# Experts of a mixture-of-experts layer: four with 32 slots share the tensor engine's array

## The chip, the cores and the metric

The kernel runs on one core of one Trainium2 chip. The metric is the device time of one execution in microseconds (us). In the text PE is the tensor engine (PEld its loading of weights), DVE the vector engine, ACT the scalar engine, POOL GpSimd and SP the sync engine, whose queue issues nearly all loads here.

## The reference

The reference is one decoder layer for 512 tokens of 1024 features: token mixing (HGRN2 and NSA attention, merged and projected), then a layer norm, then a hierarchical mixture of experts, then a layer norm. The change lies in the mixture of experts. Each token picks one of 4 groups and two of the 8 experts in it, and each of the 32 experts is a SwiGLU network from 1024 features to 512 and back:

```
(jax.nn.silu(xb @ w1[e]) * (xb @ w3[e])) @ w2[e]
```

There are 512 x 2 = 1024 choices. Routing the reference's inputs by its own rule gives experts 0 to 3 38, 37, 51 and 29 tokens; the other 28, sorted, have 81, 57, 49, 46, 41, 40, 37, 37, 35, 33, 33, 32, then 30, 30, 29, 29, 29, 27, 25, 24, 20, 19, 18, 16, 16, 14, 12, 10. An expert's three matrices are 2 MB each in float32, so that all 32 experts are 201 MB, read once.

## The kernel before

The first 760 us compute token mixing, the first norm and the router. The rest goes through the experts in **units** of 128 slots. A slot holds one token of one expert. Units -2 and -1 are experts 0, 1 and 2, 3 with 64 slots each. The other experts are sorted by their count of tokens on the chip (`sort_experts`, lines 1371 to 1431): ranks 0 and 1 have 128 slots each and are units 0 and 1 alone; ranks 2 to 27 have 64 slots each and run two to a unit, units 2 to 14. In all there are 17 units: 15 of two experts ("pairs" below) and 2 of one ("singles"). Their order is the list `ORDER` (line 75).

For each unit the loop in lines 1549 to 1578 writes out, in this order on PE: `up` (the products with w1 and w3, tile `p`); `combine` of the unit before (16 products `pcb`, which carry its rows back to the tokens); after each second unit `gather` for the next two units (64 products `pgx`, which pick the tokens' rows); transposes `pat` and `ptw`; and `down` (products with w2, tile `py`). In a pair the two experts' products stand in the two halves of the array, columns 0 to 63 and 64 to 127, by `tile_position` (line 1449). All unit products are float32; the program's one product is two matmul instructions in the trace.

SP loads each expert's weights as 12 tiles `ew` of 512 KB, four for each matrix, in the order in which PE uses them: within a unit, tile by tile and for each tile expert by expert (`load_unit`, lines 1250 to 1272). The tiles come from a pool of 36 buffers (line 158), of which 12 hold the tokens' rows and sums for the rest of the program. So 24 buffers go round: from the second unit on, each load takes the buffer of the 24th load before it, and waits until PE has made the last product with that tile. The loads also wait in turn for the one eight places before. For a unit of sorted experts SP reads each expert's number from the sorted list `ovi` (function `ev`, line 1513).

Tokens past an expert's slots go through `overflow` (line 1516), a loop over blocks of 128 slots, whose count is known only on the chip; the trace of before has no instruction of its body. The last unit's w2 comes in quarters of columns (line 1267), and its `down` and `combine` are interleaved by quarters with the sums for the last norm (lines 1637 to 1657). After that come the norm and the stores.

Of the kernel before, what the change touches and what calls it, by code (L numbers as in the profile page):

```python
# [27 lines left out]
OP = mybir.AluOpType  # L28
# [11 lines left out]
CAP = 64  # L40
SCALE = 128 ** -0.5

# columns of the constant array
# [3 lines left out]
def const_arrays():  # L47
    c = np.zeros((128, C_N), np.float32)
    p = np.arange(128)
    c[:, C_ID:C_ID + 128] = np.eye(128)  # L50
    c[:, C_TRI:C_TRI + 128] = p[:, None] <= p[None, :]
    c[:, C_IOTA:C_IOTA + 256] = np.arange(256)[None, :]
    c[:, C_VAL] = p >= 31
    # bias by distance: dist = 511 - m; bucket one-hot, then the mask row
    m = np.arange(640)
    dist = 511 - m
    n = np.maximum(dist, 1).astype(np.float64)
    large = np.minimum(16 + (np.log(n / 16) / math.log(8) * 16 + 1e-9).astype(np.int64), 31)
    bucket = np.where(np.maximum(dist, 0) < 16, np.maximum(dist, 0), large)
    oh = np.zeros((32, 1280), np.float32)  # L60
    ok = dist >= 0
    oh[bucket[ok], m[ok]] = 1.0
    oh[:, 640:] = np.where(ok, 0.0, NEG)[None, :]
    return {"cst": c, "buck": oh}
# [10 lines left out]
ORDER = [2, 3, 4, 0, 5, 6, 7, 1, 8, 9, 10, 11, 12, 13, 14]  # L75
# [4 lines left out]
class Weave:  # L80
    """Emission order: a main stream of products, with side streams put in between when what they
    wait for should be there by the tensor engine's clock."""
# [59 lines left out]
def hybrid_kernel(ctx, tc, a, out, dbg=None, stop=None):  # L142
# [52 lines left out]
    # rows 0..15 ada sh1, sc1; 16..23 c  # L195
# [6 lines left out]
    # rows 0..51 b_in[:6656]; 52..67 gates' biases; 68..83 lb logits; 84..91 norm_w; 92, 93 cmp_b1  # L202
# [7 lines left out]
    # second weights and positions of the two compressions  # L210
# [29 lines left out]
    def sigmoid(dst, src, nbias):  # L240
        # 1 / (1 + exp(-x)) as exp(-ln(1 + exp(-x)))
# [10 lines left out]
    class Block:  # L252
# [16 lines left out]
        def split1(self, sub=None):  # L269
# [3 lines left out]
            if self.early:  # L273
                # the branch's factor of each column
# [20 lines left out]
    def proj_T(b, c, ps, sh=None, sl=None, ks=range(KT)):  # L295
        # features on partitions, tokens along the free axis
# [19 lines left out]
    def run_jobs(jobs):  # L316
        """jobs: (block or None, body(block) -> generator, names of side streams to end before)"""
        blocks = [j[0] for j in jobs]

        def ahead(i):  # L320
            # what the next blocks still need, one piece at a time
# [70 lines left out]
    # layer norm of x, transposed  # L392
# [48 lines left out]
    # the first of each 32 rows: two of shift, two of scale  # L441
# [3 lines left out]
    def modulation(c):  # L445
        # 256 features of shift and scale, as rows: each over two halves of the products
# [8 lines left out]
    def modulate(c):  # L455
        # the same as columns, and their rows of h^T
# [33 lines left out]
    # lower bound: softmax over the two depth rows, row 0  # L490
# [16 lines left out]
    mod_d = dr.tile([1, 4096], F32, name="mod_d")  # L507

    def late_mod():
        accs = []  # L510
        for j in range(8):
# [13 lines left out]
            # rows side by side in the array  # L525
# [11 lines left out]
    # bias by distance, masked, as one row a head; its Toeplitz views are read back from DRAM  # L537
# [3 lines left out]
    def bias_rows():  # L541
# [23 lines left out]
        # row p of a head is read from 127 - p on: a step of 639 over 128 copies of the row  # L565
# [4 lines left out]
    # compressed values in two exact halves, stacked: high, low, high  # L570
    vcmp = cp.tile([96, 2, 128], F32R, name="vcmp")

    def compress(src, wname, b1, is_k):
# [20 lines left out]
        # windows on partitions, even and odd positions side by side  # L594
# [34 lines left out]
    # keys: per group [selected 512 | window 512], and the first blocks of both side by side  # L629
# [80 lines left out]
    def attention(hp, i):  # L710
# [55 lines left out]
        # probabilities with the keys on partitions: two blocks of keys, two heads a bank  # L766
# [18 lines left out]
        # of the compressed keys: high, high, low  # L785
# [58 lines left out]
    def c4(t):  # [128,512] as [p, tile, chunk, 32]  # L844
        return t.rearrange("p (i c j) -> p i c j", i=NT, c=4)

    def bc32(f):  # factor [128,16] over 32 tokens
# [7 lines left out]
    def hgrn_gates(h):  # L855
# [11 lines left out]
        # chunk decays and their products inside a tile of four chunks  # L867
# [3 lines left out]
        pr2 = fac[:, 5]  # [.., 0] d0 d1, [.., 1] d2 d3, [.., 2] all four  # L871
# [13 lines left out]
    def hgrn(h):  # L885
# [12 lines left out]
        # state updates  # L898
# [5 lines left out]
        # attention inside a tile, keys on partitions  # L904
# [55 lines left out]
    def on_split(hp):  # L960
        # after a pair's last tile
# [21 lines left out]
    def prep():  # L983
# [5 lines left out]
        # sh2, 1 + sc2: feature p * 8 + k on partition p  # L989
# [13 lines left out]
        # router weights with the modulation folded in  # L1003
# [91 lines left out]
    def out_piece(b, i, q, width):  # L1095
        # 256 of a tile's columns; added to x in pieces of width
# [23 lines left out]
    pk1, pk2 = S("pk1"), S("pk2")  # L1120
    onesb, strict = bfs[:, 0:128], bfs[:, 128:256]
    # scratch of [128, 4, 8] pieces
# [19 lines left out]
    def gather_first(tiles, ks=range(8)):  # L1142
        # the rows of experts 0..3: the first three tiles of tokens ahead of the last one's ranks;
        # one accumulation a bank: its second half starts where the first one's start has cleared
# [8 lines left out]
    def ln(i, z, st):  # L1153
# [32 lines left out]
        # what the experts need of the rows  # L1186
# [11 lines left out]
        # logits on partitions, even and odd features side by side  # L1198
# [9 lines left out]
        # group, two experts in it  # L1208
# [18 lines left out]
        # rank among the tokens of an expert  # L1227
# [7 lines left out]
        # slots of experts 0..3, 64 each  # L1235
# [14 lines left out]
    def load_unit(es, lo=0, hi=12, res=None, quarters=False):  # L1250
        res = res or {n: [[] for _ in es] for n in ("exp_w1", "exp_w3", "exp_w2")}
        for t in range(lo, hi):
            name = ("exp_w1", "exp_w3", "exp_w2")[t // 4]
            for x, e in enumerate(es):
                j = t % 4
                src = expert_rows(name, e)
                if t in SMALL and isinstance(e, int) and e < 2:
                    # two tiles of half the size: of those there are more than the start of the experts needs
# [6 lines left out]
                if quarters and t >= 8:  # L1265
                    # 256 columns of all rows
# [26 lines left out]
    # the routing of the last tile of tokens, the other tiles' rows in its waits  # L1293
# [25 lines left out]
    # combine weights: p(group) * softmax of the two  # L1319
# [12 lines left out]
    def one_hots(rels):  # L1332
        # rows of tokens, columns of two units' slots
# [9 lines left out]
    def gather(ph_):  # L1343
        # the rows of the slots, features on partitions, modulated
# [26 lines left out]
    def sort_experts():  # L1371
        # experts 0..3 have 64 each; of the others the two fullest have 128 and the rest 64
# [4 lines left out]
        key, rk, base, cap_, two, cnt = (srt[:, 32 * j:32 * j + 32] for j in range(6))  # L1377
# [7 lines left out]
        # the experts in the order of their units  # L1385
# [7 lines left out]
        def look(dst, table):  # L1393
            # by the expert of each choice
# [3 lines left out]
        # slots of the sorted experts  # L1398
        V.tensor_scalar(two, rk, 2.0, None, op0=OP.is_lt)
        V.tensor_scalar(cap_, two, 64.0, 64.0, op0=OP.mult, op1=OP.add)  # L1400
        V.tensor_scalar(base, rk, 64.0, -128.0, op0=OP.mult, op1=OP.add)
        V.tensor_mul(base, base, two)
        V.scalar_tensor_tensor(base, rk, 64.0, base, op0=OP.mult, op1=OP.add)
        V.tensor_scalar(base, base, 128.0, None, op0=OP.add)
# [7 lines left out]
        # tokens past an expert's slots: blocks of 128, one expert each  # L1412
# [4 lines left out]
        for j in range(1, 4):  # L1417
# [8 lines left out]
        le = S("le").rearrange("p (j e) -> p j e", j=16)  # L1426
        V.tensor_tensor(le, incl[:, None, :].to_broadcast([128, 16, 32]),
                        iota[:, 0:16].rearrange("p (j o) -> p j o", o=1).to_broadcast([128, 16, 32]), op=OP.is_le)
        V.tensor_copy(ovf[:, 32:33], incl[:, 31:32])
        V.tensor_reduce(ovf[:, 33:49].rearrange("p (j o) -> p j o", o=1), le, axis=AX.X, op=OP.add)  # L1430
        V.tensor_copy(ovi[:, 32:49], ovf[:, 32:49])

# [1 line left out]
    def weighted(rel):  # L1434
        # token rows, slot columns, weights of the choices
# [8 lines left out]
    def unit_mm(ps, lhs, n0, ws, rhs, nk):  # L1444
        # one expert, or two side by side in the array
# [36 lines left out]
    def weighted_halves(py, cs_, c0, n):  # L1482
        # columns from c0 on, weighted, in two exact halves
# [32 lines left out]
    def overflow():  # L1516
# [4 lines left out]
        with tc.For_i(0, nblk, 1) as jb:  # L1521
# [8 lines left out]
            def stream(name):  # L1530
                # a product's weights, used in the order of their loads
# [7 lines left out]
            # the last norm's sums so far  # L1539
# [5 lines left out]
    # units -2, -1: experts 0..3; 0, 1: one expert; 2..14: two  # L1545
# [3 lines left out]
    for n, u in enumerate(units):  # L1549
# [6 lines left out]
        if n == 4:  # L1556
            # of the tokens past an expert's slots
            nblk = nc.values_load_multi_w_load_instructions(
                ovi[0:1, 32:33], min_val=0, max_val=15, skip_runtime_bounds_check_because="a sum of at most 15 blocks")[1][0]
# [4 lines left out]
        if n + 1 < len(units):  # L1564
# [3 lines left out]
            elif v_ < 2:  # L1568
                es = (ev(v_),)
            else:  # L1570
                es = (ev(2 * v_ - 2), ev(2 * v_ - 1))
# [11 lines left out]
    aT, pT, cs_ = down_lhs(act, pw)  # L1583
    l3 = cp.tile([128, NT, 6], F32, name="l3")
    # sums of a tile's quarters; its halves' sums of squares, off by a shift (the first quarter's mean)
# [9 lines left out]
    def quarter_up(q):  # L1595
        # 256 columns of the last unit
# [8 lines left out]
    def quarter_add(q, y, i):  # L1605
        # the last two units' rows of a tile
# [15 lines left out]
    def close(i, half, how):  # L1622
        # norm, gain and offset of half a tile, by the engines of the three steps (two where fused)
# [34 lines left out]
    # mean; variance from the shift, less the square of what the shift missed  # L1658
# [40 lines left out]
```

## Time and profile before

| | |
|---|---|
| median of three timed runs | 1299.36 us (1298.15 to 1299.7) |
| span of the profiled execution, first to last instruction | 1295.2 us |
| PE busy | 1219.5 us, 94% |
| DVE busy | 752.6 us, 58% |
| ACT busy | 446.6 us, 34% |
| bytes moved by DMA | 297.19 MB, mean 229 GB/s |

The span is 4.2 us below the median of the timed runs, so sums made in the one are carried to the other. The page of the profile cuts the span into 40 slices of 32.4 us; the units begin in the 24th of them and fill the rest. Busy PE means that a matmul was in flight, and matmuls overlap.

### The profile page before, as it was taken

How to read it: one execution, taken by the hardware profiler on the slowest of the kernel's cores; microseconds unless marked ns; L12 is line 12 of the kernel's file. 1: busy time of each engine (PE TensorE's matmuls, PEld its weight loads, DVE VectorE, ACT ScalarE, POOL GpSimd, SP SyncE). 2: the span in 40 equal slices, each digit the busy share in tenths (PEclk: the TensorE clock that was granted, in tenths of full speed). 3: DMA queues.
4: the chain of work that ended last, by engine and by line, in shares of the span. 5: the costliest groups of instructions: out<-in, count | busy, mean ns of one | idle time of the engine just before them, and what ended most of it. 6: DMA issues, size and time to landing. Idle time of an engine off the chain costs nothing. (4 is left out here: it accounts for less than half of the span.)

```text
span 1295.2 us, 19201 instructions
## 1 busy us (share of the span) xinstructions
PE 1219.5 (94%) x6887; PEld 868.1 (67%) x6887; DVE 752.6 (58%) x1746; ACT 446.6 (34%) x937; POOL 122.1 (9%) x179
## 2 busy tenths in 40 slices
PE   6999999999999999999979879999999999999993
PEld 4788898778888888788759843554645463545542
DVE  5565888886566555324785868363534545353526
ACT  5224666673525355554132320211212121202123
POOL 3011101101110101010430220000000000000002
PEclk9999999999999999999989969999999999999997
DMA  9954423423434244353424569899999979999991
GB/s 322 298 149 126 119 62 103 130 90 94 137 104 127 81 124 123 98 167 99 130 86 175 196 240 410 334 409 408 375 339 409 409 283 397 406 409 408 408 332 66
DMA packets 140867, 297.19 MB, mean 229 GB/s; under 512 B 11100, under 2 KB 82980, under 8 KB 140769
## 3 DMA queue, kind: packets, MB, share of 16 engines
q1 hardware_dynamic: 131296, 268.57, 57.1%
q0 software_dynamic: 8704, 25.00, 6.2%
q10 hardware_dynamic: 768, 2.37, 0.5%
q8 instruction: 55, 0.90, 0.3%
q14 instruction: 44, 0.35, 0.1%
HBM read 293.76 MB, written 4.76 MB: 230 GB/s over the span
## 5 line engine op out<-in xcount | busy, mean ns | idle before, releaser
L184 PE MATMUL p<-ew,xe 128*64 128x512 f32 x960 | 209.3, 594 | 0.0
L277 DVE TENSOR_TENSOR wl<-wst,wh 128x1024 fp32r<-128x1024 f32 (+1 forms) x93 | 124.2, 1364 | 75.2 <-ACT wh L276 74.2
L184 PEld LDWEIGHTS p<-ew,xe 128*64 128x64 f32 x960 | 68.8, 137 | 137.5 <-issue 130.4
L184 PE MATMUL py<-ew,aT 128*64 128x512 f32 (+1 forms) x496 | 103.3, 568 | 3.8 <-ACT aT L1472 3.8
L276 ACT ACTIVATE wh<-wst 128x1024 fp32r<-128x1024 f32 (+1 forms) x94 | 93.0, 1030 | 29.4 <-POOL wst L275 16.6
L184 PEld LDWEIGHTS py<-ew,aT 128*64 128x64 f32 x496 | 34.2, 137 | 63.5 <-issue 51.4
L182 PE MATMUL pgx<-pm,xhh 128*128 128x256 f32 (+1 forms) x288 | 72.3, 291 | 1.9 <-DVE pm L1242 1.9
L1355 ACT ACTIVATE xe<-pgx,sm 128x256 f32<-128x256 f32 (+1 forms) x64 | 35.3, 552 | 109.6 <-PE pgx L182 109.6
L1511 DVE TENSOR_TENSOR acc<-acc,pcb 128x512 f32<-128x512 f32 x120 | 72.9, 678 | 0.0
L182 PE MATMUL pgx<-pm,xhl 128*128 128x256 f32 (+1 forms) x288 | 71.8, 290 | 0.0
L1485 DVE SCALAR_TENSOR_TENSOR y<-py,cs,g2b 128x512 f32<-128x512 f32 (+1 forms) x36 | 25.9, 718 | 78.8 <-PE py L184 68.7
L1487 ACT ACTIVATE yh<-y 128x512 fp32r<-128x512 f32 (+1 forms) x36 | 21.8, 606 | 144.3 <-DVE y L1485 131.0
L1464 DVE TENSOR_TENSOR s<-s,p 128x512 f32<-128x512 f32 x17 | 11.7, 687 | 93.0 <-PE p L184 79.2
L182 PE MATMUL pcb<-yh,pT 128*128 128x512 f32 (+1 forms) x152 | 57.4, 386 | 4.4 <-DVE s L1464 2.2
L182 PEld LDWEIGHTS pgx<-pm,xhh 128*128 128x128 f32 x288 | 57.3, 199 | 3.1 <-DVE pm L1242 2.3
L182 PEld LDWEIGHTS pgx<-pm,xhl 128*128 128x128 f32 x288 | 57.5, 200 | 0.3
L182 PE MATMUL pcb<-yl,pT 128*128 128x512 f32 (+1 forms) x152 | 54.9, 369 | 0.0
L515 POOL DMA_DIRECT2D adaw<-in_ada_w_dram x64 | 34.5, 541 | 199.8 <-PE ptp L188 45.4
L182 PE MATMUL pmg<-hh,wh 128*128 128x512 f32 x128 | 50.4, 394 | 0.0
L182 PE MATMUL psg<-hh,wh 128*128 128x512 f32 x128 | 50.3, 393 | 0.0
L182 PE MATMUL pmg<-hh,wl 128*128 128x512 f32 x128 | 49.9, 390 | 0.0
L182 PE MATMUL psg<-hl,wh 128*128 128x512 f32 x128 | 49.9, 390 | 0.0
(510 smaller groups left out, 2923.9 us busy)
## 6 DMA issues: line engine op xcount, KB each, us to landing
ew<-in_exp_w_dram SPq DMA_DIRECT2D x380, 512.0 KB, 10.1
wst<-in_w_in_dram SPq DMA_DIRECT2D x66, 512.0 KB, 4.7
adaw<-in_ada_w_dram POOLq DMA_DIRECT2D x64, 256.0 KB, 3.2
adaw<-in_ada_w_dram SPq DMA_DIRECT2D x16, 512.0 KB, 9.2
wst<-in_w_br_hg_dram SPq DMA_DIRECT2D x8, 512.0 KB, 3.7
wst<-in_w_br_nsa_dram SPq DMA_DIRECT2D x8, 512.0 KB, 4.1
wst<-in_w_out_dram SPq DMA_DIRECT2D x8, 512.0 KB, 4.9
ext_d<-ext_d POOLq DMA_DIRECT2D x1, 2560.0 KB, 17.2
```

The lines of the kernel that those rows point to most:

```text
L182: PE.matmul(o, l, r, start=start, stop=stop)
L184: PE.matmul(o, l, r, start=start, stop=stop, tile_position=pos)
L276: A.activation(wh, self.w[j], AF.Copy)
L277: (sub or V).tensor_sub(wl, self.w[j], wh.bitcast(F32))
L515: P_.dma_start(w, ada[:, k, 2048 + j * 512:2560 + j * 512])
L1355: A.activation(xe[k // 2][:, k % 2, 0:128 * u], pgx, AF.Identity, bias=sm2[:, 0, k:k + 1], scale=sm2[:, 1, k:k + 1])
L1464: V.tensor_mul(s1, s1, p3)
L1485: V.scalar_tensor_tensor(y, py, cs_, g2b[c0 // 512][:, c0 % 512:c0 % 512 + n], op0=OP.mult, op1=OP.mult)
L1487: A.activation(yh, y, AF.Copy)
L1511: V.tensor_add(acc[i][:, s_], acc[i][:, s_], pc_)
```

## The change

The constant `NOV` (20 places for overflow blocks, instead of 16) replaces an unused one. `ORDER` and the slots are new: ranks 2 to 11 keep 64 slots and stay in pairs (units 2 to 6), ranks 12 to 27 get 32 slots each and run four to a unit (units 7 to 10, "quads" below). `unit_mm` and `down` are as they were: with four experts `m` is 32, so each expert's products stand in 32 columns of the array. There are now 13 units: 7 pairs, 2 singles, 4 quads. The overflow blocks' table `le` has 20 rows, in bfloat16, instead of 16 in float32. The diff also drops comments. Its core:

```diff
-CAP = 64
+NOV = 20
...
-ORDER = [2, 3, 4, 0, 5, 6, 7, 1, 8, 9, 10, 11, 12, 13, 14]
+ORDER = [7, 0, 8, 1, 9, 2, 3, 10, 4, 5, 6]
...
-        V.tensor_scalar(two, rk, 2.0, None, op0=OP.is_lt)
-        V.tensor_scalar(cap_, two, 64.0, 64.0, op0=OP.mult, op1=OP.add)
-        V.tensor_scalar(base, rk, 64.0, -128.0, op0=OP.mult, op1=OP.add)
-        V.tensor_mul(base, base, two)
-        V.scalar_tensor_tensor(base, rk, 64.0, base, op0=OP.mult, op1=OP.add)
-        V.tensor_scalar(base, base, 128.0, None, op0=OP.add)
+        V.tensor_scalar(cap_, rk, 2.0, 64.0, op0=OP.is_lt, op1=OP.mult)
+        V.tensor_scalar(t6, rk, 12.0, 32.0, op0=OP.is_lt, op1=OP.mult)
+        V.tensor_add(cap_, cap_, t6)
+        V.tensor_scalar(t6, rk, 28.0, 32.0, op0=OP.is_ge, op1=OP.mult)
+        V.scalar_tensor_tensor(cap_, cap_, 32.0, t6, op0=OP.add, op1=OP.add)
+        V.tensor_scalar(base, rk, 64.0, 128.0, op0=OP.mult, op1=OP.add)
+        V.scalar_tensor_tensor(base, rk, 128.0, base, op0=OP.mult, op1=OP.min)
+        V.tensor_scalar(t6, rk, 32.0, 512.0, op0=OP.mult, op1=OP.add)
+        V.tensor_tensor(base, base, t6, op=OP.min)
...
-        le = S("le").rearrange("p (j e) -> p j e", j=16)
-        V.tensor_tensor(le, incl[:, None, :].to_broadcast([128, 16, 32]),
-                        iota[:, 0:16].rearrange("p (j o) -> p j o", o=1).to_broadcast([128, 16, 32]), op=OP.is_le)
+        le = S("le").bitcast(BF)[:, 0:NOV * 32].rearrange("p (j e) -> p j e", j=NOV)
+        V.tensor_tensor(le, incl[:, None, :].to_broadcast([128, NOV, 32]),
+                        iota[:, 0:NOV].rearrange("p (j o) -> p j o", o=1).to_broadcast([128, NOV, 32]), op=OP.is_le)
...
+            elif v_ < 7:
+                es = (ev(2 * v_ - 2), ev(2 * v_ - 1))
             else:
-                es = (ev(2 * v_ - 2), ev(2 * v_ - 1))
+                es = tuple(ev(4 * v_ - 16 + x) for x in range(4))
```

Three places show what moves. The first is PE at the third unit, the first of sorted experts; `p` is its two products of `up`, `py` is the `down` of the unit before it. Before, ranks 2 and 3 as a pair:

```order
L188 MATMUL pat<-cst,s_7634 128x128 x4
L188 MATMUL ptw<-cst,pw 128x128 x4
L184 MATMUL py<-ew,aT 64x512 x16
L184 MATMUL p_7893<-ew,xe 64x512 x16
L184 MATMUL p_7912<-ew,xe 64x512 x16
L182 MATMUL pcb<-yh,pT 128x512
```

Of the changed program, the same place, with ranks 12 to 15 as a quad:

```order
L188 MATMUL pat<-cst,s_7637 128x128 x4
L188 MATMUL ptw<-cst,pw 128x128 x4
L184 MATMUL py<-ew,aT 64x512 x16
L184 MATMUL p_7962<-ew,xe 32x512 x32
L184 MATMUL p_7997<-ew,xe 32x512 x32
L182 MATMUL pcb<-yh,pT 128x512
```

Each of the two products is 32 instructions on 32 rows of the output instead of 16 on 64; `combine` follows in either program.

The second is PE at the first single, the expert of rank 0, whose products are 128 wide. Before, it is the sixth unit and follows pairs:

```order
L188 MATMUL ptw<-cst,pw 128x128 x4
L184 MATMUL py<-ew,aT 64x512 x16
L182 MATMUL p_8587<-ew,xe 128x512 x8
L182 MATMUL p_8598<-ew,xe 128x512 x8
L182 MATMUL pcb<-yh,pT 128x512
```

Now it is the fourth unit:

```order
L188 MATMUL ptw<-cst,pw 128x128 x4
L184 MATMUL py<-ew,aT 32x512 x32
L182 MATMUL p_8761<-ew,xe 128x512 x8
L182 MATMUL p_8772<-ew,xe 128x512 x8
L182 MATMUL pcb<-yh,pT 128x512
```

The single now stands between two quads.

The third is SP ahead of the first loads of a quad's weights, the third unit's. Before, it reads two numbers of experts:

```order
L1514 TENSOR_LOAD ovi
L1514 ISA x2
L1514 TENSOR_LOAD ovi
L1514 ISA x2
L1270 ISA
L1270 DMA ew<-in_exp_w_dram 128x1024
```

Now it reads four, and 48 loads follow instead of 24:

```order
L1519 TENSOR_LOAD ovi
L1519 ISA x2
L1519 TENSOR_LOAD ovi
L1519 ISA x2
L1519 TENSOR_LOAD ovi
L1519 ISA x2
L1519 TENSOR_LOAD ovi
L1519 ISA x2
L1270 ISA
L1270 DMA ew<-in_exp_w_dram 128x1024
```

The four reads now stand together ahead of the loads. Over the program the reads, one for each sorted expert, and the loads, 12 for each, are as many as before.

## Rows read from the trace of the kernel before

**Rows 1.** Page, the span in 40 slices: PE busy tenths, PE clock tenths, DMA rate.

```profile
PE   6999999999999999999979879999999999999993
...
PEclk9999999999999999999989969999999999999997
...
GB/s 322 298 149 126 119 62 103 130 90 94 137 104 127 81 124 123 98 167 99 130 86 175 196 240 410 334 409 408 375 339 409 409 283 397 406 409 408 408 332 66
```

**Rows 2.** Stretches: length, busy of PE, PEld, DVE, ACT, POOL, PE clock, DMA, GB/s.

```profile
832.00:932.00 100.00, 99.19 (x474) 50.43 (x471) 49.68 (x114) 15.84 (x30) 0.00 (x0) 1.00 1.03 409
...
1072.00:1236.00 164.00, 162.33 (x850) 82.50 (x848) 76.07 (x170) 28.99 (x57) 0.00 (x0) 1.00 1.03 408
```

**Rows 3.** The same columns, the three stretches of the units with a lower rate.

```profile
816.00:832.00 16.00, 15.75 (x85) 6.66 (x85) 6.23 (x14) 3.62 (x8) 0.00 (x0) 1.00 0.70 254
934.00:952.00 18.00, 17.69 (x79) 8.50 (x79) 6.23 (x14) 4.40 (x9) 0.00 (x0) 1.00 0.70 228
1050.00:1072.00 22.00, 21.69 (x109) 11.87 (x109) 6.23 (x14) 6.55 (x13) 0.00 (x0) 1.00 0.62 205
```

**Rows 4.** Waits of SP's queue, 780 to 1260 us: total, times, longest.

```profile
SPq L1270 <- DMA ew<-in_exp_w_dram: 168.0, 236, 1.2
SPq L1270 <- PE py L184: 50.8, 40, 11.2
SPq L1270 <- PE py L182: 30.5, 8, 13.4
```

**Rows 5.** Timeline of PE, a pair: start, length, instructions merged.

```profile
851.39 13.90 PE L184 MATMUL p<-ew,xe 128*64 128x512 f32 x64
...
878.06 7.09 PE L184 MATMUL py<-ew,aT 128*64 128x512 f32 x32 [0.31 <-ACT aT L1472]
884.98 13.90 PE L184 MATMUL p<-ew,xe 128*64 128x512 f32 x64
```

**Rows 6.** Stretches, products of gather alone: length, PE busy, clock, DMA, GB/s.

```profile
868.00:877.00 9.00, 7.84 (x64) 1.00 1.03 409
1225.00:1234.00 9.00, 7.26 (x64) 1.00 1.03 411
```

**Rows 7.** Timeline of PE, the first single.

```profile
910.92 14.00 PE L182 MATMUL p<-ew,xe 128*128 128x512 f32 x32
...
937.48 7.13 PE L182 MATMUL py<-ew,aT 128*128 128x512 f32 x16 [0.31 <-ACT aT L1472]
```

**Rows 8.** Timeline of PE, products of 32 columns, four side by side.

```profile
16.59 1.93 PE L184 MATMUL pg<-adaw,cT 128*32 128x256 f32 x32
```

**Rows 9.** Timeline of DVE, small steps of the sorting.

```profile
787.86 0.17 DVE L1399 TENSOR_SCALAR srt<-srt 128x32 f32<-128x32 f32 x1
...
788.37 0.19 DVE L1402 TENSOR_TENSOR srt<-srt 128x32 f32<-128x32 f32 x1
788.60 0.19 DVE L1403 SCALAR_TENSOR_TENSOR srt<-srt 128x32 f32<-128x32 f32 x1
```

**Rows 10.** Page, DMA issues: count, KB each, median us to landing.

```profile
ew<-in_exp_w_dram SPq DMA_DIRECT2D x380, 512.0 KB, 10.1
```

**Rows 11.** Timeline of the end: last ordinary loads, last unit but one, last unit, last quarter.

```profile
1209.98 25.93 SPq L1270 DMA_DIRECT2D ew<-in_exp_w_dram  x21
...
1222.19 0.50 PE L182 MATMUL pcb<-yh,pT 128*128 128x512 f32 x1
...
1241.42 13.90 PE L184 MATMUL p<-ew,xe 128*64 128x512 f32 x64
...
1267.32 1.95 PE L184 MATMUL py<-ew,aT 128*64 128x256 f32 x16
```

**Rows 12.** Stretches of PE around the experts' start: length, busy, clock, DMA, GB/s.

```profile
744.00:748.00 4.00, 1.78 (x9) 0.78 1.04 403
...
752.00:756.00 4.00, 2.82 (x19) 0.50 1.03 411
...
764.00:768.00 4.00, 4.00 (x18) 0.66 0.00 0
768.00:772.00 4.00, 4.00 (x22) 1.00 0.70 238
```

More of the change, by code (lines that the diff above doesn't have):

```diff
@@ L1376, in sort_experts @@
         srt = S("srt")
-        key, rk, base, cap_, two, cnt = (srt[:, 32 * j:32 * j + 32] for j in range(6))
+        key, rk, base, cap_, t6, cnt = (srt[:, 32 * j:32 * j + 32] for j in range(6))
         V.tensor_copy(cnt, pcnt[:, 0:32])
@@ L1425, in sort_experts @@
         V.tensor_add(oslots, oslots, far)
-        le = S("le").rearrange("p (j e) -> p j e", j=16)
-        V.tensor_tensor(le, incl[:, None, :].to_broadcast([128, 16, 32]),
-                        iota[:, 0:16].rearrange("p (j o) -> p j o", o=1).to_broadcast([128, 16, 32]), op=OP.is_le)
+        le = S("le").bitcast(BF)[:, 0:NOV * 32].rearrange("p (j e) -> p j e", j=NOV)
+        V.tensor_tensor(le, incl[:, None, :].to_broadcast([128, NOV, 32]),
+                        iota[:, 0:NOV].rearrange("p (j o) -> p j o", o=1).to_broadcast([128, NOV, 32]), op=OP.is_le)
         V.tensor_copy(ovf[:, 32:33], incl[:, 31:32])
-        V.tensor_reduce(ovf[:, 33:49].rearrange("p (j o) -> p j o", o=1), le, axis=AX.X, op=OP.add)
-        V.tensor_copy(ovi[:, 32:49], ovf[:, 32:49])
+        V.tensor_reduce(ovf[:, 33:33 + NOV].rearrange("p (j o) -> p j o", o=1), le, axis=AX.X, op=OP.add)
+        V.tensor_copy(ovi[:, 32:33 + NOV], ovf[:, 32:33 + NOV])
     def weighted(rel):
@@ L1558, in hybrid_kernel @@
             nblk = nc.values_load_multi_w_load_instructions(
-                ovi[0:1, 32:33], min_val=0, max_val=15, skip_runtime_bounds_check_because="a sum of at most 15 blocks")[1][0]
+                ovi[0:1, 32:33], min_val=0, max_val=NOV - 1,
+                skip_runtime_bounds_check_because="a sum of fewer blocks than NOV")[1][0]
         act = up(xe, (n % 2) * 128, ws)
```

## The prediction

> **What bounds the kernel now.** I read the page's slices first: from the 25th on, where the experts' units are, PE shows 9 in all but the last and the DMA rate sits near 409 GB/s, with dips in the 26th, the 29th and 30th, and the 33rd [rows 1]. Two resources are close to full, and the question is which one gives way. Over 832 to 932 us and 1072 to 1236 us the rate is 409 and 408 GB/s with PE busy all the time [rows 2]; in three stretches it falls to 254, 228 and 205 GB/s, with PE still busy all the time [rows 3]. So PE never waits for weights, while loads do wait. Whom they wait for stands in the waits of SP's queue: besides turns behind other loads, 50.8 us for products `py` of pairs and 30.5 us for those of singles [rows 4]. A load waits for the last product of `down`, because that frees its buffer. **PE is the bound, by a little, and the loads lose time where it holds their buffers.**
>
> The ledger of one unit shows how small that margin is. A pair begins `up` at 851.39 us, its `down` ends where the next `up` begins, at 884.98 us: 33.6 us with a gather in it [rows 5], of which 7.84 us are the gather for two units [rows 6]. Without one it is 25.8 us. A single takes 14.00 us for `up` and 7.13 us for `down` against 13.90 and 7.09 us of a pair [rows 5, 7]: to PE, every unit costs the same. To the loads it does not: a tile of 524,288 bytes at 409 GB/s is 1.28 us, so a single's 12 tiles are 15.4 us, a pair's 24 are 30.8 us and a quad's 48 are 61.5 us. A pair with its half of a gather (29.7 us of PE) balances its loads; a single (also 29.7 us) is 14 us dearer than its loads. The two late dips begin while PE is in a single, and last 18 and 22 us.
>
> **The change part by part.** *Units.* PE loses four units. Of each go two products of `up`, one `down`, 16 of `combine`, the transposes and half a gather, 29.7 us in all if a quad costs what a pair costs: 4 x 29.7 = 119 us of PE. The nearest row for a quad is the modulation at the start, whose 32 instructions of 32 columns, 256 wide, four different moving tiles side by side, take 1.93 us [rows 8]. That is 8 groups of 0.24 us, or 0.48 us at 512 columns at most; a pair's `up` is 32 groups of two in 13.90 us, 0.43 us each (two groups are one step of 128 features, 0.87 us, and two steps use up a tile of each expert). So a quad's `up` is 13.9 to 15.4 us, and its PE time with half a gather 30 to 32 us, half of its loads' 61.5 us. From both sides it is safe: even at no gain over two pairs' products (twice 13.9 + 6.9, so 20.8 us more) a quad needs about 51 us of PE, still under its loads.
>
> *The bound changes hands.* Then loads are the bound, and PE's 119 us are mostly not gained. What can be gained is what the loads lose today. By 1 - rate/409 the late dips cost 18 x 0.443 = 8.0 us and 22 x 0.499 = 11.0 us, 19.0 us together [rows 3]. The dip at 816 us costs 16 x 0.379 = 6.1 us; it comes from `down` of unit -1, behind the wait for the sorting, and but for the sorting nothing ahead of it changes, so I leave it in.
>
> *Do the singles stall the loads again?* A quad ahead of each changes that. PE waits for the quad's last tile, so it enters a single with no backlog, about 1.7 us (two steps of 0.87 us) after that tile has landed. In the single, its `up` tiles are freed as they are used; only its four w2 tiles are held till `down`, which leaves at least 20 of the 24 buffers for the next quad. Those carry the loads to (12 - 1.3 + 20) x 1.28 = 39 us after the start of the single, and PE is back at freeing the next quad's first tiles after 33.8 + 1.7 = 35.5 us. The margin of about 4 us hides it; it stays hidden if PE is up to that much late. Between quad and single together PE needs 30 + 30 us, the loads 77 us. In the old order the singles followed pairs that PE was behind on, with nearly all buffers taken.
>
> *Sorting.* Nine small DVE steps in place of six, 0.17 us each by their durations and about 0.2 us apart [rows 9], and a table `le` of 640 elements instead of 512: 0.8 us more. Combine and `gather` of unit -1 follow in the queues, and the dip at 816 us with them: at most 0.8 us later, at least nothing; I take 0.8. The four reads of an expert's number on SP instead of two come while earlier loads are in flight (a load lands 10.1 us after its issue [rows 10]), which covers them. Without that cover each would show as a gap in the loads.
>
> *The end.* The last ordinary load is issued by 1209.98 + 25.93 = 1235.9 us [rows 11] and lands 10.1 us later, at 1246.0 us [rows 10]. It moves to 1246.0 - 19.0 + 0.8 = 1227.8 us. Its 24th predecessor, the last w3 tile of the last unit but one, lands 24 x 1.28 = 30.8 us earlier, at 1197.0 us; PE, which now waits for it, ends that `up` two steps later, at 1198.7 us. From there PE is the bound again, for its chain from the first `pcb` to the end of the last `up` takes 1241.42 + 13.90 - 1222.19 = 33.1 us [rows 11] against 30.8 us of loads. The last `up` ends at 1231.8 us instead of 1255.3 us: **23.5 us earlier**. The tail behind it, from 1255.3 us to the end, is the same work, 39.9 us. Its quarters of w2 still come in time: the last one is used 12.0 us after `up` [rows 11], at 1243.8 us, and the loads behind the last ordinary one (8 tiles and the norm's two tiles of 128x1024, 10 x 1.28 = 12.8 us) are there by 1240.6 us. By the span: 1295.2 - 23.5 = 1271.7 us.
>
> *The clock.* A new cost appears. Where PE waits, its granted clock falls from 2.4 GHz to 1.2 GHz: at 744 us, after a stretch with PE busy 1.78 of 4 us, it goes to 0.50, is still there with PE busy 2.82 of 4 us, and is back at 1.00 at 768 us, after PE has worked steadily from about 760 us [rows 12]. In a quad PE works 1.7 of each 5.1 us, so I expect 0.5 there. It costs nothing as long as the loads are behind; half speed makes a step of four tiles 3.5 us, under 5.1. It costs up to 4 us where PE comes out of such waiting into work of its own: in a single (the margin above) and ahead of the final 33.1 us. I take 2 us, between 0 and 8. The Trainium skill (TensorE: Matmul & The Clock Gate, HAM oscillation) states that a PE that waits on DMA between bursts of matmuls is throttled back each time and runs the next burst cold; it speaks against a change that makes PE wait. The trace agrees in the stretch at 744 us. By that rule alone, with every run of work after a wait cold for its half, the sum would be the first rival's 1294 us; by the row, with the clock back after some 8 us, it is the 2 us that I take.
>
> The sum: 1299.4 (median; the profiled span is 4.2 us less) - 23.5 + 2 = **1277.9**, say 1278 us.
>
> **The rivals.** *The clock takes more.* If the low clock lasts through the final chain of 33.1 us, half speed adds 33 us less what the last loads allow; with half of it slow, 16 us: 1294 us. For it: the low clock at 744 us lasted 20 us with PE partly busy. Against it: the last three units are pairs, in whose `up` PE works 1.74 us of each 2.56 us of loads, and steady work brought the clock back within some 8 us. *Two abreast only.* If four experts of 32 columns run like two pairs, PE per quad and single is 51 + 30 = 81 us against 77 us of loads, twice in a row: up to 2 x 4 = 8 us, 1286 us. Against it stands the modulation's row. *The singles still stall.* If PE enters them late, the 19.0 us return: 1297 us. *It goes further:* if the early dip goes too, 1272 us. *Slower: the overflow loop.* A 32-slot expert with over 32 tokens costs one pass of `overflow`, run alone at the end: 24 loads of 256 KB through two buffers, at least 24 x 0.64 = 15.4 us, with a unit's 29.7 us of PE: 45 us or more, 1323 us and up, decided by the first expert past its slots. The fullest of the sixteen has 30 tokens by the reference's routing, so three tokens would have to change sides. As improbable is one at a time in the array (4 x 0.87 us a step, a quad about 93 us of PE, four of them 31 us over their loads each: near 1400 us).
>
> **How the numbers follow.** Forecast 0.70; clock 0.10; two abreast 0.07; singles stall 0.04; further 0.03; overflow or one at a time 0.06. The range of 8 in 10 takes the forecast with its bounds (the sorting's 0 to 0.8, the clock's 0 to 8 us, two or three for the dips read from mean rates), two abreast and the further gain: 1270 to 1288 us; most of the clock rival and the slow ones are left out. About 0.2%, 2.6 us, is what a measurement of this kernel can tell from no change. Faster: forecast, clock, two abreast, further, 0.90; the stalled singles, 1297, count as the same, 0.04; slower 0.06.
>
> **What would show it.** In the changed profile: `p` on 128x32 with 32 groups in about 14 us when no weights are missing; PE's waits naming `ew` loads, which hardly exist now; a rate near 409 GB/s without the late dips, the one at 816 us still there; PE's clock below 1.00 in the quads; the last ordinary load issued near 1218 us. It would be wrong if a dip stands beside `p` of 128 columns, if PE's last 33 us are longer at a lower clock, or if lines of the overflow loop appear.

## The result and the profile after

| | before | after |
|---|---|---|
| median | 1298.76 us (4 runs) | 1277.27 us (4 runs, 1275.47 to 1279.8) |
| span of the profiled execution | 1295.2 us | 1274.4 us |
| PE busy | 1219.5 us, 94% | 1176.6 us, 92% |

The ratio of the times is 0.9846, with an interval of 0.9823 to 0.9868: faster by some 20 us. 1278 us were predicted. Each run below has its ratio to runs of before that were taken beside it; their medians are 1296.9 us (19 runs), 1297.13 us (9) and 1296.81 us (17), lower than the 1298.76 us of the table.

The page's slices of the changed kernel answer to [rows 1]: PE in tenths, its clock in tenths, the DMA rate.

```profile
PE   5999999999999999999979969999999899899993
...
PEclk9999999999999999999999979999999999999997
...
GB/s 324 295 152 139 120 52 117 104 87 129 112 109 142 45 174 100 92 147 156 132 66 182 79 301 361 297 411 408 409 409 409 409 409 408 409 409 407 403 346 68
```

The rate is flat from the 27th slice on: the late dips (339 in the 30th, 283 in the 33rd) are gone. The dip in the 26th slice is still there and deeper than before, 297 against 334. PE shows an 8 now in some slices, and no slice of the experts has a clock below 9 but the first and the last.

The waits, 780 to 1260 us, answer to [rows 4]: who waited for whom, total in us, times, longest. Those of PE's weight loading (PEld) and of its products (PE), for tiles of weights:

```profile
PEld p L184 <- DMA ew<-in_exp_w_dram: 85.1, 109, 1.8
...
PEld py L184 <- DMA ew<-in_exp_w_dram: 28.8, 35, 1.2
...
PE p L184 <- DMA ew<-in_exp_w_dram: 14.4, 58, 0.9
...
PE py L184 <- DMA ew<-in_exp_w_dram: 5.2, 22, 0.3
```

Before, the same view has no such row of PE, and these of PEld:

```profile
PEld p L184 <- DMA ew<-in_exp_w_dram: 5.1, 18, 0.3
...
PEld py L184 <- DMA ew<-in_exp_w_dram: 2.6, 9, 0.3
```

The same view of SP's queue, after:

```profile
SPq L1270 <- DMA ew<-in_exp_w_dram: 218.2, 297, 1.9
SPq L1270 <- PE py L184: 23.3, 14, 13.4
...
SPq L1270 <- PE py L182: 0.2, 1, 0.2
```

The two sides have changed places. The loads' wait for `py` of singles went from 30.5 to 0.2 us, that for `py` of pairs and quads from 50.8 to 23.3 us, and PE's weight loading now waits for tiles 144 times (27 times before), for the most part while products are still in flight. PE's products stood still for tiles 80 times, 19.6 us in all.

The end, as a timeline (start, length, instructions merged), answers to [rows 11]: the ordinary loads, the last steps of the last unit but one, the first `pcb` behind them, the last unit, the last quarter.

```profile
740.91 478.57 SPq L1270 DMA_DIRECT2D ew<-in_exp_w_dram  x356
...
1198.68 1.93 PE L184 MATMUL p<-ew,xe 128*64 128x512 f32 x6 [0.20 <-DMA ew<-in_exp_w_dram]
1200.54 0.50 PE L182 MATMUL pcb<-yh,pT 128*128 128x512 f32 x1
...
1219.79 14.78 PE L184 MATMUL p<-ew,xe 128*64 128x512 f32 x64
...
1246.54 1.95 PE L184 MATMUL py<-ew,aT 128*64 128x256 f32 x16
```

The last ordinary load is issued by 740.91 + 478.57 = 1219.5 us (before: 1235.9), the last `up` ends at 1234.6 us (before: 1255.3), and the end follows 39.8 us behind it, as before (39.9).

Spans differ by a few us already in the 760 us ahead of the experts. So the runs below are also compared by one stretch within the execution: from the start of `pcnt`, the product that counts the tokens behind the first `up`, to the end of the ordinary loads. "Stretch" in the text means this one.

| run | time, us | ratio to before, interval | `pcnt`, us | loads end, us | stretch, us |
|---|---|---|---|---|---|
| before | 1298.76 | | 780.02 | 1235.91 | 455.89 |
| after | 1277.27 | 0.9846, 0.9823 to 0.9868 | 777.93 | 1219.48 | 441.55 |
| `up` of quads twice | 1279.25 | 0.9855, 0.9833 to 0.9877 | 782.00 | 1223.49 | 441.49 |
| two quads | 1279.27 | 0.9856, 0.9836 to 0.9876 | 779.13 | 1220.98 | 441.84 |
| singles after pairs | 1300.08 | 1.0021, 1.0007 to 1.0035 | 777.37 | 1239.44 | 462.07 |
| last expert first | 1277.42 | 0.9838, 0.9813 to 0.9863 | 779.24 | 1221.30 | 442.06 |
| tables later | 1274.50 | 0.9816, 0.9799 to 0.9834 | 779.43 | 1216.66 | 437.23 |
| gather after down | 1272.03 | 0.9812, 0.9788 to 0.9836 | 776.52 | 1213.48 | 436.96 |
| both | 1271.38 | 0.9806, 0.9792 to 0.9821 | 780.36 | 1214.29 | 433.93 |
| both, in the kernel before | 1295.64 | 0.9993, 0.9984 to 1.0003 | 777.70 | 1230.93 | 453.23 |

### The profile page after: what moved, and what is told of

Its sections match the earlier page's. It is cut to its first block, busy times and chain, and to the rows that moved or that the text cites. A ratio compares the mean times of both kernels' runs of the same rounds, so it can differ in the third digit from the quotient of the medians.

```text
span 1274.4 us, 18563 instructions
## 1 busy us (share of the span) xinstructions
PE 1176.6 (92%) x6663; PEld 813.2 (64%) x6663; DVE 697.5 (55%) x1621; ACT 425.5 (33%) x897; POOL 123.4 (10%) x179
## 5 line engine op out<-in xcount | busy, mean ns | idle before, releaser
L184 PE MATMUL p<-ew,xe 128*32 128x512 f32 (+1 forms) x960 | 209.0, 599 | 14.9 <-DMA ew<-in_exp_w_dram 14.4
L184 PEld LDWEIGHTS p<-ew,xe 128*32 128x32 f32 (+1 forms) x960 | 55.1, 122 | 166.7 <-DMA ew<-in_exp_w_dram 85.4
L184 PE MATMUL py<-ew,aT 128*32 128x512 f32 (+2 forms) x496 | 96.6, 570 | 7.8 <-DMA ew<-in_exp_w_dram 5.2
L184 PEld LDWEIGHTS py<-ew,aT 128*32 128x32 f32 (+1 forms) x496 | 27.1, 122 | 70.5 <-issue 34.2
L182 PE MATMUL pgx<-pm,xhh 128*128 128x256 f32 (+1 forms) x224 | 58.3, 299 | 1.5 <-DVE pm L1242 1.5
L182 PE MATMUL pgx<-pm,xhl 128*128 128x256 f32 (+1 forms) x224 | 57.6, 296 | 0.0
L1516 DVE TENSOR_TENSOR acc<-acc,pcb 128x512 f32<-128x512 f32 x88 | 53.5, 679 | 0.0
L182 PE MATMUL psg<-hh,wl 128*128 128x512 f32 x128 | 49.9, 390 | 0.0
L182 PE MATMUL pmg<-hl,wh 128*128 128x512 f32 x128 | 49.8, 389 | 0.0
L182 PE MATMUL pcb<-yh,pT 128*128 128x512 f32 (+1 forms) x120 | 44.5, 381 | 5.1 <-DVE s L1469 2.9
## 6 DMA issues: line engine op xcount, KB each, us to landing
ew<-in_exp_w_dram SPq DMA_DIRECT2D x380, 512.0 KB, 10.1
```

The lines of the kernel that those rows point to most:

```text
L182: PE.matmul(o, l, r, start=start, stop=stop)
L184: PE.matmul(o, l, r, start=start, stop=stop, tile_position=pos)
L1516: V.tensor_add(acc[i][:, s_], acc[i][:, s_], pc_)
```

## Who is the bound: three experiments

**More work for PE.** Edit, in `unit_mm` (the sums are halved behind it):

```diff
-                mm(ps[m * x:m * x + m, :], lhs(k)[:, n0 + m * x:n0 + m * x + m], rhs(ws[x], k), k == 0, k == nk - 1,
-                   pos=(0, m * x) if m < 128 else None)
+                for r in range(2 if m == 32 else 1):
+                    mm(ps[m * x:m * x + m, :], lhs(k)[:, n0 + m * x:n0 + m * x + m], rhs(ws[x], k), k == 0 and r == 0,
+                       k == nk - 1 and (m > 32 or r == 1), pos=(0, m * x) if m < 128 else None)
```

> In the four quads every product of `up` is made twice (the sums are halved again behind it), so PE gets 15.4 us more work in each quad, 61.6 us in all, by the 0.48 us of a group of four that the changed kernel's first quad showed (11.79 us for 98 instructions). Loads stay as they are. Theory (behind the change the loads are the bound in the quads, PE has some 30 us to spare in each): with 24 buffers in turn the last landing does not move, 1277 us, at most 1281. Rival (PE's products still set the time, and the change gained because there are fewer of them): 1277 + 61.6 = 1339 us.

Measured: 1279.25 us, and the stretch is 441.49 us, against 441.55 without the edit. The timeline of PE in the first quad and in the second:

```profile
829.80 27.75 PE L184 MATMUL p<-ew,xe 128*32 128x512 f32 x256
...
904.98 27.75 PE L184 MATMUL p<-ew,xe 128*32 128x512 f32 x256
```

Twice the products fill 27.75 us with no wait that the timeline shows, so 13.9 us were added to each quad, 55.5 us in all (the 15.4 us of the expectation were too much: the row of 11.79 us it rests on held short waits for tiles). They cost nothing that shows. PE is not the bound in the quads.

**Fewer loads, after and before.** Edit of the changed kernel; in the kernel before the same with `7 <= v_ <= 12`:

```diff
-            ws = load_unit(es, quarters=n + 2 == len(units))
+            if 7 <= v_ <= 9:
+                ws = load_unit(es, 0, 8)
+                ws["exp_w2"] = [[w3[0]] * 4 for w3 in ws["exp_w3"]]
+            else:
+                ws = load_unit(es, quarters=n + 2 == len(units))
```

> The changed kernel, but in the first three quads (ranks 12 to 23) w2 is not loaded: `down` multiplies with the first w3 tile of each expert instead, so the output of those experts is left out of what is right. 48 loads of 512 KB fewer, 48 x 1.28 = 61.5 us at 409 GB/s; PE's work is the same. Theory (loads are the bound): the time falls by most of 61.5 us; some comes back as waits for buffers, since the singles then follow quads of 41 us of loads instead of 61.5: by a count of buffers 1229 us (1216 to 1240). Rival (PE is still the bound): 1275 to 1277 us.

> The kernel before, with the same 48 loads left out (w2 of ranks 12 to 23, units 7 to 12, replaced by the first w3 tile of each expert). Theory of the prediction's first step (before the change PE was the bound, by a little, and loads waited for PE to free buffers): 1297 to 1299 us, no gain, the rate of the loads falls instead. Rival (the loads were the bound before, too): at least 40 of the 61.5 us come off, 1258 us or less.

Measured: the changed kernel falls to 1229.36 us, by 47.9 us, and the kernel before stays at 1297.25 us (ratio 1.0003, 0.9993 to 1.0012). Stretch of the kernel before with 48 loads fewer: length, busy of PE, PEld, DVE, ACT, POOL, PE clock, DMA, GB/s.

```profile
1020.00:1236.00 216.00, 213.76 (x1073) 110.88 (x1073) 102.37 (x232) 39.55 (x77) 0.00 (x0) 1.00 0.76 288
```

The rate falls to 288 GB/s and PE works through as it did [rows 2]. The same 48 loads are worth nothing before and 47.9 us after: **PE was the bound, now the loads are.**

## What the gain depends on: order and number

**The same quads in another order.**

```diff
-ORDER = [7, 0, 8, 1, 9, 2, 3, 10, 4, 5, 6]
+ORDER = [2, 0, 3, 1, 7, 8, 9, 10, 4, 5, 6]
```

> The changed kernel with another order alone: ORDER = [2, 0, 3, 1, 7, 8, 9, 10, 4, 5, 6], so both singles follow pairs and all four quads come behind them. The same products and loads. Theory (a gain needs loads that are never held up; a single costs PE 29.7 us for 15.4 us of loads, and only a quad ahead of it leaves PE without backlog): the loads stall at the singles again and the time lost there can't be made up, since the loads are the bound in the quads: by a count of buffers the last landing comes 24 us later than in the changed kernel, 1301 us (1294 to 1305), no faster than before. Rival (the gain is the 119 us of products that PE no longer makes, wherever they stand): 1277 to 1280 us.

Measured: 1300.08 us, no faster than before. Stretches of this run, columns as above: two ahead of the quads, and the quads and pairs behind them.

```profile
866.00:880.00 14.00, 13.69 (x87) 11.17 (x86) 3.79 (x7) 5.68 (x11) 0.00 (x0) 1.00 0.53 209
...
920.00:940.00 20.00, 19.69 (x106) 14.85 (x105) 6.49 (x11) 5.68 (x11) 0.00 (x0) 1.00 0.54 209
...
1000.00:1235.00 235.00, 214.03 (x1008) 79.50 (x1008) 59.89 (x129) 26.56 (x52) 0.00 (x0) 1.00 1.03 409
```

At both singles the rate falls to 209 GB/s while PE is busy; from 1000 us on it is 409 and PE has 21 us to spare that nobody can use. What PE saves lies behind the singles, where the loads are the bound, and nothing is gained by it.

**Half the quads.** Ranks 20 to 27 alone get 32 slots; ranks 12 to 19 stay in pairs (the constants of `sort_experts` and the quads' index into the sorted list follow):

```diff
-ORDER = [7, 0, 8, 1, 9, 2, 3, 10, 4, 5, 6]
+ORDER = [11, 0, 12, 1, 2, 3, 4, 5, 6, 7, 8, 9, 10]
...
-            elif v_ < 7:
+            elif v_ < 11:
```

> Half of the change: only ranks 20 to 27 get 32 slots and make two quads, ranks 12 to 19 stay in pairs; ORDER puts one quad ahead of each single and all nine pairs behind. 15 units, PE saves 59 us of products instead of 119. Theory (the gain is what the loads lost at the singles, and stops there): 1277 to 1281 us, as with four quads. Rival (each quad brings its share of the gain): 1288 us.

Measured: 1279.27 us, stretch 441.84 us. Two quads, one ahead of each single, bring the whole gain within the intervals; the other two add nothing that can be told from zero. What counts is that no load is held up at a single.

## The clock in the quads

```diff
-            for x in range(len(ws)):
+            for x in reversed(range(len(ws))):
```

(the same in `down`; the loads keep their order)

> The changed kernel with the experts of a unit taken in reverse order in `up` and `down`, while the loads keep their order. PE then waits for the last of four tiles before it begins a step of a quad and makes two steps, 1.9 us, in one go every 5.1 us, as the prediction had it, instead of one instruction after each landing. Prediction's seventh step: the granted clock falls in the quads, to about 0.5, and the time grows by 0 to 8 us, 1277 to 1285. Rival (waits of some 3 us between such bursts don't take the clock down; the changed kernel's 1.00 in the quads had nothing to do with the order): 1.00 in the quads and 1277 us.

Measured: 1277.42 us. The last quad in the changed kernel, two stretches:

```profile
1100.00:1106.00 6.00, 5.30 (x25) 1.04 (x19) 1.08 (x4) 0.00 (x0) 0.00 (x0) 1.00 1.03 410
1106.00:1112.00 6.00, 4.66 (x18) 0.79 (x16) 0.00 (x0) 0.60 (x1) 0.00 (x0) 1.00 1.03 407
```

The timeline of PE there:

```profile
1101.95 1.04 PE L184 MATMUL p<-ew,xe 128*32 128x512 f32 x2 [0.23 <-DMA ew<-in_exp_w_dram]
1103.23 1.04 PE L184 MATMUL p<-ew,xe 128*32 128x512 f32 x2 [0.24 <-DMA ew<-in_exp_w_dram]
1104.50 2.40 PE L184 MATMUL p<-ew,xe 128*32 128x512 f32 x12 [0.23 <-DMA ew<-in_exp_w_dram]
```

The same place with the last expert first, the stretches:

```profile
1100.00:1106.00 6.00, 2.80 (x16) 0.47 (x16) 2.88 (x11) 0.00 (x0) 0.00 (x0) 0.68 1.03 410
1106.00:1112.00 6.00, 3.64 (x16) 0.59 (x16) 0.00 (x0) 0.60 (x1) 0.00 (x0) 0.50 1.03 409
```

Its timeline of PE:

```profile
1096.13 1.92 PE L184 MATMUL p<-ew,xe 128*32 128x512 f32 x16 [2.35 <-DMA ew<-in_exp_w_dram]
1101.25 2.80 PE L184 MATMUL p<-ew,xe 128*32 128x512 f32 x16 [3.20 <-DMA ew<-in_exp_w_dram]
1106.37 3.64 PE L184 MATMUL p<-ew,xe 128*32 128x512 f32 x16 [2.32 <-DMA ew<-in_exp_w_dram]
...
1117.30 1.92 PE L184 MATMUL p<-ew,xe 128*32 128x512 f32 x16 [1.38 <-DMA ew<-in_exp_w_dram]
1122.41 3.47 PE L184 MATMUL p<-ew,xe 128*32 128x512 f32 x16 [3.18 <-DMA ew<-in_exp_w_dram]
1127.53 1.92 PE L184 MATMUL p<-ew,xe 128*32 128x512 f32 x16 [1.65 <-DMA ew<-in_exp_w_dram]
```

As the program stands, each landing lets one expert's instructions go, and the rest follow with the fourth tile: PE pauses for 0.2 us at a time, is busy for 4.7 to 5.3 of 6 us, and keeps its clock. In reverse order the work comes in one burst about every 5.1 us. Then the granted clock falls to 0.50, 1.2 GHz, and comes back, by turns: the same 16 instructions take 1.92, 2.80 and 3.64 us, later 1.92 and 3.47 us, and of the eight bursts of this `up` four take 1.92 us. Even 3.64 us fit into 5.1 us, and the time doesn't change. The Trainium skill (TensorE: Matmul & The Clock Gate, HAM oscillation) has a PE that waits on DMA between bursts run each burst cold. The second run agrees for half of its bursts, with up to 3.64 us for 1.92, and the changed kernel shows that the order of the instructions decides whether there is such a burst.

## The early dip

The prediction left it at 6.1 us. Stretches of before and of after, columns as above:

```profile
808.00:814.00 6.00, 5.08 (x39) 4.78 (x40) 5.65 (x10) 2.04 (x4) 0.00 (x0) 1.00 1.02 408
814.00:820.00 6.00, 5.75 (x45) 4.66 (x46) 0.69 (x1) 3.57 (x8) 0.00 (x0) 1.00 0.54 216
820.00:826.00 6.00, 6.00 (x32) 2.00 (x30) 0.75 (x1) 0.22 (x1) 0.00 (x0) 1.00 0.67 221
826.00:832.00 6.00, 6.00 (x32) 2.00 (x30) 4.79 (x12) 1.04 (x2) 0.00 (x0) 1.00 1.00 378
```

```profile
808.00:814.00 6.00, 6.00 (x38) 5.89 (x37) 4.24 (x8) 1.96 (x4) 0.00 (x0) 0.72 1.03 409
814.00:820.00 6.00, 5.75 (x44) 4.71 (x44) 0.69 (x1) 3.66 (x8) 0.00 (x0) 1.00 0.11 45
820.00:826.00 6.00, 6.00 (x32) 1.88 (x32) 0.75 (x1) 0.14 (x1) 0.00 (x0) 1.00 0.72 225
826.00:832.00 6.00, 6.00 (x60) 1.82 (x56) 4.74 (x12) 1.12 (x2) 0.00 (x0) 1.00 0.99 371
```

By 1 - rate/409 of each row, 814 to 832 us lost 6.0 us of loads before and 8.6 us after. PE waits for DVE's product `s` ahead of its last `pcb`, first the row of before, then of after:

```profile
808.92 0.50 PE L182 MATMUL pcb<-yh,pT 128*128 128x512 f32 x1 [2.20 <-DVE s L1464]
```

```profile
807.52 0.50 PE L182 MATMUL pcb<-yh,pT 128*128 128x512 f32 x1 [2.93 <-DVE s L1469]
```

The nine sorting steps show there as 0.7 us. Behind the wait the clock is at 0.72 and `gather` of unit -1 takes 9.3 us (808.12 to 817.38) instead of 7.8 (809.52 to 817.30). It isn't shown that this part is the change's: the kernel before with fewer loads shows 0.72 behind a wait of 2.23 us and 9.2 us of `gather`, and of the runs with the changed sorting three more show 9.3 us, but the one with the singles after pairs shows 1.00 and 7.8 us behind a wait of 2.91 us. The wait alone doesn't settle whether the clock falls there; what does is open.

Two edits shorten the dip. **The tables of the overflow blocks later** (`overflow_tables` is what stood in `sort_experts` from `need` on):

```diff
             todo = down(act, w_now, pw)
+        if n == 1:
+            overflow_tables(*srt_)
```

> The changed kernel with one edit: the tables of the overflow blocks (from `need` on, 4.9 us on DVE from 789.55 to 794.43 us) are written out behind `down` of unit -1 instead of inside the sorting, where DVE's product `s` of unit -1 was queued behind them and PE waited 3.4 us for it, with its clock at 0.72 in the 6 us behind. Theory (the early dip is PE coming late to unit -1's `down`, and every us of it reaches the end, since the loads are the bound from there): the wait goes and the clock stays at 1.00, the dip from 814 us is 3.4 to 5 us shorter and the time 1272 to 1274 us. Rival (the dip depends on the loads' own start, or its gain is lost at the end, where PE's last two pairs decide): 1277 us.

**`gather` behind `down`, in unit -1 alone:**

```diff
-        if nxt:
+        if nxt and n != 1:
             xe = gather(hots)
         if n + 1 < len(units):
             todo = down(act, w_now, pw)
+        if nxt and n == 1:
+            xe = gather(hots)
```

> The changed kernel with one edit: for unit -1 alone, `gather` is written behind `down` instead of ahead of it, so that the eight w2 tiles of that unit are freed up to 9 us earlier. Theory (the early dip is the wait of loads for those tiles): the dip from 814 us becomes shorter; by a count of buffers 2.5 us at least, 9 us at most, and the end comes as much earlier: 1268 to 1275 us. Rival (what comes off there is lost again because PE enters the first quad without rows, or because the loads are held by `down` of unit -2): 1277 us.

**Both, in the changed kernel and in the kernel before:**

> The changed kernel with the two edits to the early dip together: the overflow tables behind `down` of unit -1, and `gather` behind that `down`. Theory (both shorten the same dip of some 9 us, so their gains of 2.8 and 5.2 us, medians of the single runs against 1277.3, add up as long as the dip lasts): 1268 to 1271 us. Rival (one covers the other: the loads then wait for something else, or PE for rows): 1272 us, as with `gather` moved alone.

> The kernel before with the same two edits. Theory (PE is the bound there, so a shorter stall of the loads buys nothing by itself; what comes off is only PE's own wait of 2.6 us for `s`, where it waits for DVE): 1294 to 1297 us, 0 to 3 us less than before. Rival (a shorter early dip brings the end forward there too): 1289 us, 8 us less.

Measured: the stretch is 4.3 us shorter with the tables moved, 4.6 us with `gather` moved, 7.6 us with both. The times are 1274.50, 1272.03 and 1271.38 us: by these the tables add 0.65 us to what `gather` alone brings, by the stretch 3.0 us. The experts begin at times that differ by some us from run to run, and the stretch leaves that out. The times alone settle less: that of the tables is just past the 1272 to 1274 us expected, with an interval that overlaps that of the changed kernel, and that of both lies between the theory (1268 to 1271 us) and its rival (1272 us). With both, the dip is gone:

```profile
814.00:820.00 6.00, 6.00 (x44) 4.68 (x41) 3.57 (x9) 2.89 (x6) 0.00 (x0) 1.00 1.03 410
820.00:826.00 6.00, 6.00 (x54) 4.15 (x56) 5.73 (x21) 2.57 (x5) 0.00 (x0) 1.00 1.03 410
826.00:832.00 6.00, 6.00 (x60) 1.82 (x56) 0.71 (x2) 0.60 (x1) 0.00 (x0) 1.00 1.00 397
```

In the kernel before the same edits close the same dip, and the loads slow down a little later instead:

```profile
814.00:820.00 6.00, 6.00 (x52) 6.00 (x51) 4.93 (x17) 3.69 (x7) 0.00 (x0) 1.00 1.03 411
820.00:826.00 6.00, 6.00 (x32) 2.46 (x32) 3.77 (x13) 1.13 (x2) 0.00 (x0) 1.00 1.02 397
...
874.00:880.00 6.00, 6.00 (x32) 2.00 (x30) 0.94 (x2) 0.00 (x0) 0.00 (x0) 1.00 0.96 356
```

Its time of 1295.64 us can't be told from before. A load that comes sooner is worth something only where loads are the bound. The version with both edits, 1271.38 us, is the fastest that computes everything; the 1272 us that the prediction gave for a run without the early dip were about right.

## Why the prediction was right, and where it was not

**The bound, before.** Right: 48 loads fewer gave nothing there.

**A quad costs PE no more than a pair.** Right, at the lower end: 13.9 us for an `up` of 128 instructions, as the run with twice the products shows. That the bound changes hands and most of PE's 119 us aren't gained: right. Half of the quads gave the same time, and 55.5 us more work for PE cost nothing.

**The late dips go, the singles stay clear.** Right in mechanism. The singles' waits fell from 30.5 to 0.2 us. The rival in which they still stall was put at 1297 us; with the singles after pairs it came about, at 1300.08 us.

**The size of that step** is what failed. By the sum the last ordinary load was to come 19.0 - 0.8 = 18.2 us earlier; the stretch became 455.89 - 441.55 = 14.3 us shorter. Of the 3.9 us, 1.8 are the early dip, which grew by 2.6 us instead of the sorting's 0.8. PE's wait for `s` there grew by 0.7 us, as priced; the prediction had no term for the low clock behind that wait, 9.3 us of `gather` instead of 7.8. About 0.6 us more is a rate of 403 to 407 GB/s from 1160 to 1220 us. Some 1.5 us are left. The stretch isn't quite the same work in the two executions, before and after:

```profile
780.02:1235.91 455.89, 448.54 (x2238) 228.14 (x2238) 224.82 (x521) 81.64 (x157) 0.00 (x0) 1.00 0.98 386
```

```profile
777.93:1219.48 441.55, 414.56 (x2038) 179.30 (x2038) 170.06 (x397) 60.51 (x117) 0.00 (x0) 1.00 1.01 401
```

By length and rate that is 176.0 MB before and 177.1 MB after, about two tiles more, some 2 to 3 us by these rounded rates. That is enough for the rest.

**The end.** From the last ordinary load to the end of the program it became (1295.2 - 1235.9) - (1274.4 - 1219.5) = 4.4 us shorter; the sum had 23.5 - 18.2 = 5.3. PE left the last `up` but one at 1200.5 us (1198.7 predicted) and took 34.0 us from there to the end of the last `up` (33.1 predicted, the row of 14.78 us instead of 13.90). The prediction has PE as the bound again there, with each load landing 10.1 us after its issue. For the last ordinary load of the changed kernel, the issues between 1218.9 and 1219.6 us show more:

```profile
ew<-in_exp_w_dram SPq DMA_DIRECT2D x1, 512.0 KB, 13.5
```

It landed near 1232.6 us, and the last `up` ended at 1234.6 us, 2.0 us behind it. At its usual 13.9 us that `up` would have ended at 1233.7 us. So the last tile still set the end, by 0.9 us, where the prediction had PE's own chain. Before, the last load's landing took 10.9 us and `up` ended 8.9 us behind it.

**The clock.** Wrong for this order: 0.5 was expected in the quads and 1.00 is there. The row it rested on, at 744 us, has PE waiting for ACT and DVE (3.1 and 3.2 us at the longest between 735 and 766 us), not for loads. The premise failed, work in bursts; where the bursts are made, the clock goes to 0.50 for part of them and a step of four tiles then takes up to 3.64 us (3.5 predicted), at no cost that shows.

**The total.** Measured within the execution, 14.3 + 4.4 = 18.7 us came off where the sum had 23.5. The 2 us set aside for the clock covered part of the miss, and the profiled execution began its experts 2.1 us sooner than that of before (by `pcnt`), which no step had. The base was high, too: the forecast starts from 1299.36 us, the median of three runs, and from the 1296.9 us of 19 later ones the same steps give 1275.4 us. So that 1277.27 us came within 1 us of 1278 is in part luck. The ratio's interval, 17 to 23 us, holds the 18.7 us and the forecast's 23.5 - 2 = 21.5 us, but not 23.5.

## What to carry to other kernels

When two resources are close to full, taking work from the one that is the bound gains only until the other takes over; ask how little has to be taken, and at which places. Here two units at the right places did what four did, and four at the wrong places did nothing. To find the bound, take away the same thing on both sides, some loads or some products, and see which of the two moves the end.

## What the runs showed of the hardware

Four float32 products of 32 columns side by side take the time of one that fills the array: 27.75 us for 64 groups of four is 0.434 us a group, 13.90 us for 32 groups of two is 0.434, and a single's 14.00 us for 32 instructions is 0.438 [rows 5, 7]. For a product of 32 columns alone the nearest rows are the changed kernel's two instructions of one expert, 1.04 us: with 0.60 us for one (the page's mean) the second starts some 0.44 us behind the first. By that estimate four at a time are about four times as fast as one at a time. The Trainium skill (TensorE: Matmul & The Clock Gate, Measured speedup vs the span model) gives 2.38 for three of 32 columns and 512 wide, and has no row for four; the measurement here lies well above and is taken.
